# First stage of a hybrid backbone step: load order, filter network kept in one piece, h modulated on ScalarE

## The chip, the cores and the metric

The kernel runs on one core of a Trainium2 chip. The metric is the device time of one execution in microseconds (us); the time before is the median of three runs.

## The reference

One layer of an inference step for 640 tokens of width 1024: 128 context tokens ("prompt", row 0 of `x_tok`) and 512 latent tokens. What the first stage has to produce is the modulated input and the Hyena filters:

```
mod   = silu(cond) @ ada_w + ada_b                  # 6 x 1024: shift1, scale1, gate1, ...
h     = x * (1 + scale1) + shift1
proj  = h @ w_in                                    # q, two gates, v, g, Hyena's three, two mixing gates
hf    = sin(freq0*(z@w1+b1)); hf = sin(freq1*(hf@w2+b2)); hf = sin(freq2*(hf@w3+b3))
filt  = (hf @ w4) * window                          # forward and backward filters, 1024 channels
K     = spectrum(filt)                              # later used as U * K in the long convolution
```

After it come the HGRN2 scan, the short and long convolutions, two projections, the mixing, a layer norm, a SwiGLU network of width 2816 and a second layer norm. All in float32; matmuls are done as three passes over high and low parts (`hi*hi`, `hi*lo`, `lo*hi`).

## The kernel before

The first stage is written out as a list of short tokens, `PLAN`, which `start()` walks through; a scheduler then places the instructions on the five engines, in an order that follows the list where nothing is missing. Each engine runs its own instructions in that fixed order, so one that waits holds up all behind it. All loads stand in SyncE's queue (`SPq`), but for small parameters, which GpSimd issues (token `p`).

The tokens that matter here: `x0` to `x4` load 128 tokens each, `T0` to `T4` transpose them on TensorE and copy the result out of PSUM (`xT`). `mlp` is the filter network (`filter_mlp`): three layers, each a small matmul and then four VectorE steps and a sine on ScalarE (`sin_layer`). `L0` to `L3` load the last filter matrix `w4` and the window for 256 channels (`kern_load`), `A0` to `A3` (`kern_a`) make the filter (matmuls `ks`, product with the window `af`, high and low parts `abh`, `abl`), `B0` to `B3` (`kern_b`) its spectrum by matmuls with the table `kth`, `ktl`, which `k0` to `k2` load and split (`ktab`). `D0` to `D3` load two pieces of 1 MB of `ada_w` for one block of the modulation, `M0` to `M3` multiply and transpose them (`ada_mods`, result `modT`). `h0` to `h7` (`make_h`) modulate 128 rows of x and split them into `hTh` and `hTl`; `HMOD` says which engine modulates (V is VectorE, S is ScalarE), `HSUB` which engine forms the low part (G is GpSimd). `W0` to `W3` store the spectra (`kern_store`, issued from ScalarE's queue). `V0` and `V1` are the first two units of `h @ w_in` (`v_unit`), `m` and the tokens after it the next stage, whose first matmul writes `ma` (line 675).

Buffers tie these together. `xs` has three buffers for five loads, `win` two (the input of the filter network, `zT`, takes one of them first), `araw` three, `raw` three (the `kt` loads use them before the weights do), `af` two. The spectra of blocks 0 and 1 are kept in the buffers that later hold the high (`wh`) and low (`wl`) parts of the weights, three of each, until they have been stored. A PSUM bank of the tag `x` (five) goes from use to use.

Of the kernel before, what the change touches and what calls it, by code (L numbers as in the profile page):

```python
# [12 lines left out]
AF = mybir.ActivationFunctionType  # L13
# [4 lines left out]
P = 128  # L18
# [99 lines left out]

PLAN = """x0 k0 L0 k1 x4 k2 p mlp t L1 T0 x3 T4 A0 x2 D0 T2 A1 x1 L2 B0 M0 T1 D2 A2 M2 T3 h0 L3 B1 D1 A3 h1 B2 M1 D3 h2 h3 M3 h4 W2 W0 h5 h6 h7 W1 q V0 e0 B3 g0 W3 V1 m w0 e2 10 20 g1 50 11 60 g2 70 21 30 40 w1 w2 61 51 52 12 71 Q8 62 22 g3 w3 13 41 g4 53 72 Q9 42 31 63 w4 g5 23 14 w5 73 Z4 Q10 43 32 g6 w6 64 24 15 54 74 Q11 33 65 25 44 16 26 55 75 Q12 Z5 g7 34 w7 66 45 56 17 76 Q13 35 67 46 g8 27 57 w8 18 77 Z6 Q14 g9 g10 36 w9 28 19 68 37 29 58 78 Q15 69 47 59 w10 79 Q16 38 110 210 Z7 g11 610 49 111 510 39 48 w11 211 g12 611 112 w12 212 710 Q17 g13 511 711 Q18 410 113 w13 311 612 Z8 310 411 512 712 Q19 513 213 613 412 713 312 413 313 Z9"""
HMOD = "SVSSVSSS"  # L120
HSUB = "GVVVVGVG"
# [42 lines left out]
def body(tc, I, O):  # L164
# [5 lines left out]
    def act(out, in_, func, bias=0.0, scale=1.0):  # L170
        r = S.activation(out, in_, func, bias=bias, scale=scale)  # L171
        if func in TABLE_FUNCS:
            if last_table[0] is not None:
                tc.add_manual_dep(
                    r.ins, last_table[0].name,
                    mybir.DependencyInfo(mybir.DependencyClass.NoSync, mybir.DependencyReason.DATA),
                    reason="table order")
            last_table[0] = r.ins
        return r

    def tt(out, a, b, op, eng=None):
# [271 lines left out]

    def x_transpose(t, xs):
        for q in range(2):
            ps = sc_bank(f"xT{t}_{q}")
            for k in range(4):
                PE.transpose(ps[:, k * P:k * P + P], xs[:, (4 * q + k) * P:(4 * q + k + 1) * P], ident)
            for i in range(2):
                cpy("x", 2 * t + q, xT.tiles[2 * q + i][:, :, t * P:t * P + P],  # L460
                    ps[:, i * 256:i * 256 + 256].rearrange("p (k t) -> p k t", k=2))
# [14 lines left out]


    def sin_layer(psrc, i, nm):
        a = se.tile([P, HT], F32, tag="af", bufs=2, name=f"sa{nm}")
        V.tensor_scalar(a, psrc, fpar[:, 3 + i:4 + i], fpar[:, 6 + i:7 + i], ALU.add, ALU.mult)  # L480
        k = sp.tile([P, HT], F32, tag="ko", bufs=1, name=f"sk{nm}")
        V.tensor_scalar(k, a, MAGIC, None, ALU.add)
        V.scalar_tensor_tensor(a, k, MAGIC, a, ALU.subtract, ALU.subtract)
        V.tensor_scalar(a, a, HALF, -HALF, ALU.min, ALU.max)
        act(a, a, AF.Sin, scale=-TWO_PI)
        return a
# [243 lines left out]
    def start():  # L730
# [1062 lines left out]
```

## Time and profile before

| what | us |
|---|---|
| median of three runs | 1416.66 (1416.07 to 1417.04) |
| the profiled execution | 1414.7 |
| its span, first to last instruction | 1412.6 |
| TensorE matmuls busy | 1371.9 (97%) |
| VectorE busy | 995.5 (70%) |
| ScalarE busy | 620.8 (44%) |
| GpSimd busy | 63.4 (4%) |

The page divides the span into 40 slices. TensorE is full in nearly all of them but the first two, which are the stage of this change: 5 and 9 tenths, with weight loads at 2 and 6. GpSimd works almost only there (4, 3 and 3 tenths in the first three slices). In the page PE is TensorE, PEld its weight loads, DVE VectorE, ACT ScalarE, POOL GpSimd; a busy PE is not PE at its peak, since matmuls overlap.

### The profile page before, as it was taken

What the parts mean: (1) busy time and instruction counts of PE and PEld (TensorE: products, weight loads), DVE (VectorE), ACT (ScalarE), POOL (GpSimd) and SP (SyncE); (2) the same over time, 40 slices, a digit from 0 to 9 for tenths busy, and PEclk for the clock granted to TensorE, in tenths of its full rate; (3) what the DMA queues carried; (4) which work ended last, traced back from release to release, by engine and by line L of the source; (5) the groups of instructions that cost most, each with busy time, mean ns of one, the idle gap of its engine ahead of it and who ended that gap; (6) DMA issues with size and microseconds to landing.
All of it is one profiled execution on the core that took longest, in us unless ns stands there. A gap on an engine that the chain in (4) does not pass through costs nothing. (4 is left out here: it accounts for less than half of the span.)

```text
span 1412.6 us, 23432 instructions
## 1 busy us (share of the span) xinstructions
PE 1371.9 (97%) x9513; PEld 1291.7 (91%) x9513; DVE 995.5 (70%) x1751; ACT 620.8 (44%) x1011; POOL 63.4 (4%) x56
## 2 busy tenths in 40 slices
PE   5989999999999999999999999998999999999997
PEld 2689889999999999999999999987999999998886
DVE  6886776656889743558887786568987776765426
ACT  3655554432322211546656655327654444542121
POOL 4330000020000000000000000000000000000003
PEclk9999999999999999999999999999999999999999
DMA  7944665675333374433222223552553213267211
GB/s 244 339 139 145 214 212 180 194 245 176 94 86 98 112 231 142 137 94 90 78 87 72 77 60 108 192 172 84 163 149 106 81 58 117 80 210 263 75 60 75
DMA packets 198857, 195.64 MB, mean 138 GB/s; under 512 B 7582, under 2 KB 155774, under 8 KB 197981
## 3 DMA queue, kind: packets, MB, share of 16 engines
q1 hardware_dynamic: 194860, 179.75, 40.6%
q0 software_dynamic: 2160, 9.15, 1.7%
q10 hardware_dynamic: 1728, 5.24, 0.9%
q8 instruction: 74, 1.21, 0.4%
q14 instruction: 35, 0.28, 0.1%
HBM read 162.91 MB, written 31.21 MB: 137 GB/s over the span
## 5 line engine op out<-in xcount | busy, mean ns | idle before, releaser
L182 DVE TENSOR_TENSOR wl<-raw,wh 128x1024 fp32r<-128x1024 f32 x96 | 117.3, 1223 | 133.3 <-ACT wh L358 132.5
L358 ACT CAST wh<-raw 128x1024 fp32r<-128x1024 f32 x90 | 94.1, 1049 | 220.1 <-PE pb L612 41.0
L1431 PE MATMUL fo<-wh,act 128*128 128x512 f32 (+1 forms) x440 | 130.6, 380 | 0.0
L1431 PEld LDWEIGHTS fo<-wh,act 128*128 128x128 f32 x440 | 81.2, 188 | 15.9
L1431 PE MATMUL fo<-wl,act 128*128 128x512 f32 (+1 forms) x220 | 83.4, 379 | 0.0
L612 PE MATMUL hy<-hTh,wh 128*128 128x320 f32 x256 | 79.6, 311 | 0.0
L612 PE MATMUL hy<-hTh,wl 128*128 128x320 f32 x256 | 79.1, 309 | 0.0
L612 PE MATMUL hy<-hTl,wh 128*128 128x320 f32 x256 | 79.1, 309 | 0.0
L612 PE MATMUL f<-hTh,wh 128*128 128x320 f32 x224 | 70.7, 316 | 0.0
L612 PE MATMUL f<-hTl,wh 128*128 128x320 f32 x224 | 69.7, 311 | 0.0
L612 PE MATMUL f<-hTh,wl 128*128 128x320 f32 x224 | 69.2, 309 | 0.0
L182 POOL TENSOR_TENSOR y<-y,gb 128x512 f32<-128x512 f32 x8 | 11.6, 1452 | 891.2 <-ACT y L171 890.9
L1431 PEld LDWEIGHTS fo<-wl,act 128*128 128x128 f32 x220 | 41.3, 188 | 7.9
L612 PEld LDWEIGHTS hy<-hTh,wh 128*128 128x128 f32 x256 | 48.1, 188 | 0.0
L612 PEld LDWEIGHTS hy<-hTl,wh 128*128 128x128 f32 x256 | 48.1, 188 | 0.0
L612 PEld LDWEIGHTS hy<-hTh,wl 128*128 128x128 f32 x256 | 48.1, 188 | 0.0
L171 ACT ACT_TABLE_LOAD x36 | 46.2, 1283 | 1.4 <-PEq L1777 0.7
L715 PE MATMUL v<-wh,hTl 128*128 128x256 f32 x160 | 45.1, 284 | 1.4 <-POOL hTl L182 1.4
L715 PE MATMUL v<-wl,hTh 128*128 128x256 f32 x160 | 44.8, 284 | 1.6 <-DVE wl L182 1.6
L715 PE MATMUL v<-wh,hTh 128*128 128x256 f32 x160 | 44.6, 283 | 0.0
L612 PEld LDWEIGHTS f<-hTl,wh 128*128 128x128 f32 x224 | 42.2, 188 | 0.0
L612 PEld LDWEIGHTS f<-hTh,wh 128*128 128x128 f32 x224 | 42.2, 188 | 0.0
(2292 smaller groups left out, 4699.3 us busy)
## 6 DMA issues: line engine op xcount, KB each, us to landing
raw<-in_w_in SPq DMA_DIRECT2D x52, 512.0 KB, 4.0
araw<-in_ada_w SPq DMA_DIRECT2D x20, 1024.0 KB, 6.2
rm<-in_w_in SPq DMA_DIRECT2D x28, 512.0 KB, 4.6
rp<-in_ffn_w_in SPq DMA_DIRECT2D x24, 512.0 KB, 5.8
raw<-in_ffn_w_out SPq DMA_DIRECT2D x22, 512.0 KB, 4.7
rf<-in_ffn_w_in SPq DMA_DIRECT2D x18, 512.0 KB, 5.0
sd<-my SPq DMA_DIRECT2D x28, 320.0 KB, 2.3
kk<-kd SPq DMA_DIRECT2D x20, 256.0 KB, 2.7
```

The source lines that it names most:

```text
L171: r = S.activation(out, in_, func, bias=bias, scale=scale)
L182: return (eng or V).tensor_tensor(out=out, in0=a, in1=b, op=op)
L358: (V.tensor_copy if HIE[i] == "V" else S.copy)(hi, raw)
L612: r = PE.matmul(ps[:, 0:HT], w[a][:, k, :], x[b][:, k, c0:c0 + HT], start=k == 0 and i == 0, stop=k == kt - 1 and i == 2)
L715: PE.matmul(ps[:, (t - t0) * 256:(t - t0) * 256 + 256], hT[b][:, k, t * P:t * P + P], w[a][:, k % 4, :], start=k == 0 and i == 0, stop=k = ...
L1431: PE.matmul(ps, x(t, b, k0 + kk), w[a][:, kk, :], start=first and kk == 0 and i == 0, stop=last and kk == nk - 1 and i == 2)
```

## The change

`PLAN` is rewritten from its start to `B3`; from `g0` on it is the same. `x4` is loaded second and the filter network comes before the tables `k0` to `k2`, which follow the first pair of `ada_w` loads. The blocks of the modulation are loaded and multiplied in the order 0, 2, 1, 3 as before, but block 2 comes ahead of the second filter block's spectrum, and h0 to h3 ahead of block 1. `HMOD` names ScalarE for all eight blocks of h. The casts of the table all go to ScalarE. Four instructions get an explicit place on their engine: x0's first transpose after the second layer's matmul `f2`, the casts of the table after the third layer's first sine, and the first block's sums `wsd` after the second layer's last VectorE step. `filter_mlp` therefore does the transposes of x0 itself.

```diff
--- before.py
+++ after.py
@@ -116,8 +116,8 @@
     return {k: np.ascontiguousarray(v) for k, v in c.items()}
 
 
-PLAN = """x0 k0 L0 k1 x4 k2 p mlp t L1 T0 x3 T4 A0 x2 D0 T2 A1 x1 L2 B0 M0 T1 D2 A2 M2 T3 h0 L3 B1 D1 A3 h1 B2 M1 D3 h2 h3 M3
...
-HMOD = "SVSSVSSS"
+PLAN = """x0 x4 L0 p mlp L1 x3 T4 t D0 A0 k0 k1 k2 T3 x2 x1 T2 A1 M0 D2 T1 B0 L2 M2 D1 h0 h1 h2 h3 A2 B1 L3 D3 M1 M3 B2 A3
...
+HMOD = "SSSSSSSS"
 HSUB = "GVVVVGVG"
 WSUB = "VGGVVGGG"
 TAILPOS = 1
@@ -139,7 +139,7 @@
 PHB = 2
 GB = 3
 PSA2 = dict(mm=("mm", 4), sc=("x", 4), o=("x", 4), tr=("x", 4))
-COPIES = {'x': 'SSVSSSSSSS', 'h': 'SSSSSSSV', 'm': 'SV', 'k': 'VSS', 'w': 'SVVS', 'v': 'VSSS', 'a': 'SSSSSSSSSVVSSSSSSSSS', 'o': 'SSSSSSSSVSSS'}
+COPIES = {'x': 'SSVSSSSSSS', 'h': 'SSSSSSSV', 'm': 'SV', 'w': 'SVVS', 'v': 'VSSS', 'a': 'SSSSSSSSSVVSSSSSSSSS', 'o': 'SSSSSSSSVSSS'}
 ASUB = "GVVVGVGVGGGGVGVGVVVG"
 KSUB = "GGG"
 HP = False
@@ -177,6 +177,13 @@
                     reason="table order")
             last_table[0] = r.ins
         return r
+
+    def order_after(ins, prev):
+        if prev is not None:
+            tc.add_manual_dep(
+                ins.ins, prev.ins.name,
+                mybir.DependencyInfo(mybir.DependencyClass.NoSync, mybir.DependencyReason.DATA),
+                reason="issue order")
 
     def tt(out, a, b, op, eng=None):
         return (eng or V).tensor_tensor(out=out, in0=a, in1=b, op=op)
@@ -451,11 +458,13 @@
         SY.dma_start(xs, x_tok[t])
         return xs
 
-    def x_transpose(t, xs):
+    def x_transpose(t, xs, after=None):
         for q in range(2):
             ps = sc_bank(f"xT{t}_{q}")
             for k in range(4):
-                PE.transpose(ps[:, k * P:k * P + P], xs[:, (4 * q + k) * P:(4 * q + k + 1) * P], ident)
+                x = PE.transpose(ps[:, k * P:k * P + P], xs[:, (4 * q + k) * P:(4 * q + k + 1) * P], ident)
+                if q == 0 and k == 0:
+                    order_after(x, after)
             for i in range(2):
                 cpy("x", 2 * t + q, xT.tiles[2 * q + i][:, :, t * P:t * P + P],
                     ps[:, i * 256:i * 256 + 256].rearrange("p (k t) -> p k t", k=2))
@@ -475,14 +484,16 @@
         tt(hTl[:, k, :], xT[:, k, :], f32(hTh[:, k, :]), ALU.subtract, G if HSUB[k] == "G" else V)
 
 
+    net = {}
+
     def sin_layer(psrc, i, nm):
         a = se.tile([P, HT], F32, tag="af", bufs=2, name=f"sa{nm}")
         V.tensor_scalar(a, psrc, fpar[:, 3 + i:4 + i], fpar[:, 6 + i:7 + i], ALU.add, ALU.mult)
         k = sp.tile([P, HT], F32, tag="ko", bufs=1, name=f"sk{nm}")
         V.tensor_scalar(k, a, MAGIC, None, ALU.add)
         V.scalar_tensor_tensor(a, k, MAGIC, a, ALU.subtract, ALU.subtract)
-        V.tensor_scalar(a, a, HALF, -HALF, ALU.min, ALU.max)
-        act(a, a, AF.Sin, scale=-TWO_PI)
+        net["clamp", nm] = V.tensor_scalar(a, a, HALF, -HALF, ALU.min, ALU.max)
+        net["sin", nm] = act(a, a, AF.Sin, scale=-TWO_PI)
         return a
 
     hf_hi = sp.tile([P, T], F32R, name="hf_hi")
@@ -490,7 +501,7 @@
     kth = sp.tile([P, 2304], F32R, name="kth")
     ktl = sp.tile([P, 2304], F32R, name="ktl")
 
-    def filter_mlp():
+    def filter_mlp(xs0):
         ps = sc_bank("f1")
         for hf in range(2):
             PE.matmul(ps[hf * ORD:hf * ORD + ORD, 0:HT], w1, zT[:, hf * HT:hf * HT + HT], start=True, stop=True)
@@ -498,8 +509,9 @@
         ps = sc_bank("f2")
         for hf in range(2):
             cs = slice(hf * ORD, hf * ORD + ORD)
-            PE.matmul(ps[cs, 0:HT], w2[cs], h1[cs], start=True, stop=True)
+            net["f2"] = PE.matmul(ps[cs, 0:HT], w2[cs], h1[cs], start=True, stop=True)
         h2 = sin_layer(ps[:, 0:HT], 1, "2")
+        x_transpose(0, xs0, net["f2"])
         V.memset(hf_lo[ORD:P, :].bitcast(F32), 0.0)
         for hf in range(2):
             ps = sc_bank(f"f3_{hf}")
@@ -514,7 +526,7 @@
         cs = slice(i * 768, i * 768 + 768)
         raw = wp.tile([P, 768], F32, tag="raw", bufs=RAW_BUFS, name=f"kt{i}")
         SY.dma_start(raw, I["kt"][:, cs])
-        cpy("k", i, kth[:, cs], raw)
+        order_after(S.copy(kth[:, cs], raw), net["sin", "31"])
         tt(ktl[:, cs], raw, f32(kth[:, cs]), ALU.subtract, G if KSUB[i] == "G" else V)
 
     def kern_load(cc):
@@ -531,8 +543,10 @@
         c0 = cc * 256
         w4, win, skp = loaded
         wsd = se.tile([P, 2, 256], F32, tag="wsd", name=f"wsd{cc}")
-        tt(wsd[:, 0], w4[:, 0], w4[:, 1], ALU.add)
-        tt(wsd[:, 1], w4[:, 0], w4[:, 1], ALU.subtract)
+        for i, op in enumerate((ALU.add, ALU.subtract)):
+            x = tt(wsd[:, i], w4[:, 0], w4[:, 1], op)
+            if cc == 0:
+                order_after(x, net["clamp", "2"])
         whi = se.tile([P, 2, 256], F32R, tag="whi", name=f"whi{cc}")
         cpy("w", cc, whi, wsd)
         whl = se.tile([P, 2, 256], F32R, tag="whl", bufs=1, name=f"whl{cc}")
@@ -597,13 +611,6 @@
     def kern_store(cc, out):
         for t, f, n in out:
             KQ.dma_start(kd[cc, :, f:f + n], t)
-
-    def order_after(ins, prev):
-        if prev is not None:
-            tc.add_manual_dep(
-                ins.ins, prev.ins.name,
-                mybir.DependencyInfo(mybir.DependencyClass.NoSync, mybir.DependencyReason.DATA),
-                reason="issue order")
 
     def dense_fm(w, x, half, ps, kt=KT, after=None):
         c0 = half * HT
@@ -773,11 +780,7 @@
 
         for tok in PLAN.split():
             if tok == "mlp":
-                if HP:
-                    with tc.high_priority():
-                        filter_mlp()
-                else:
-                    filter_mlp()
+                filter_mlp(xs[0])
                 continue
             step(tok[0], int(tok[1:] or 0))
 
```

Lines of `PLAN` are cut at `h4`; the rest of each is the same.

The order of instructions on an engine, as the scheduler set it, differs at these places. First SyncE's queue of loads at the start; `xs` are pieces of x, `kt` of the table, `w4` and `win` a filter block's matrix and window, `araw` pieces of `ada_w`. Before:

```order
L516 DMA kt0_141<-in_kt 128x768
L524 DMA w4_0_145<-in_filt_w4 64x2x256 x2
L527 DMA win0_148<-in_win 128x5x256
L516 DMA kt1_150<-in_kt 128x768
L451 DMA xs4_154<-in_x_sample 128x1024
L516 DMA kt2_156<-in_kt 128x768
L524 DMA w4_1_224<-in_filt_w4 64x2x256 x2
L527 DMA win1_227<-in_win 128x5x256
L451 DMA xs3_243<-in_x_sample 128x1024
L451 DMA xs2_316<-in_x_sample 128x1024
```

Now:

```order
L458 DMA xs4_141<-in_x_sample 128x1024
L536 DMA w4_0_143<-in_filt_w4 64x2x256 x2
L539 DMA win0_146<-in_win 128x5x256
L536 DMA w4_1_217<-in_filt_w4 64x2x256 x2
L539 DMA win1_220<-in_win 128x5x256
L458 DMA xs3_222<-in_x_sample 128x1024
L405 DMA araw0_0_247<-in_ada_w 128x4x512
L405 DMA araw0_1_249<-in_ada_w 128x4x512
L528 DMA kt0_308<-in_kt 128x768
L528 DMA kt1_312<-in_kt 128x768
L528 DMA kt2_316<-in_kt 128x768
L458 DMA xs2_334<-in_x_sample 128x1024
```

The three `kt` moved behind the first two `araw`, x4 and the second filter block's loads moved ahead, and x2, the last of the first piece, now follows the `kt`.

GpSimd at the end of the stage; `wl1` and `wl2` are low parts of weights for the v units, `hTl3` the low part of the last pair of h's blocks, `abl3` the low parts of the last filter block. Before:

```order
L182 TENSOR_TENSOR abl2_3_554<-af2_3_551,abh2_3_553 128x512
L182 TENSOR_TENSOR wl1_926<-raw1_923,wh1_925 128x1024
L182 TENSOR_TENSOR wl2_932<-raw2_929,wh2_931 128x1024
L182 TENSOR_TENSOR abl3_0_702<-af3_0_697,abh3_0_701 128x512
L182 TENSOR_TENSOR hTl2_873<-xT2_131,hTh2_872 128x640
L182 TENSOR_TENSOR abl3_4_740<-af3_4_737,abh3_4_739 128x512
L182 TENSOR_TENSOR hTl3_889<-xT3_132,hTh3_888 128x640
```

Now:

```order
L189 TENSOR_TENSOR abl2_3_612<-af2_3_609,abh2_3_611 128x512
L189 TENSOR_TENSOR abl3_0_831<-af3_0_826,abh3_0_830 128x512
L189 TENSOR_TENSOR hTl2_873<-xT2_131,hTh2_872 128x640
L189 TENSOR_TENSOR hTl3_889<-xT3_132,hTh3_888 128x640
L189 TENSOR_TENSOR abl3_4_869<-af3_4_866,abh3_4_868 128x512
L189 TENSOR_TENSOR wl1_926<-raw1_923,wh1_925 128x1024
L189 TENSOR_TENSOR wl2_932<-raw2_929,wh2_931 128x1024
```

The two `wl` moved behind `hTl3` and the last `abl3`.

ScalarE's queue in the same part; `kd` are the stores of the spectra, `ko1` those of block 1, `wh0` to `wh2` high parts of weights, `hTh` high parts of h. Before:

```order
L185 CAST hTh1_842<-xT1_130 128x640
L185 CAST abh2_4_562<-af2_4_560 128x512
L599 DMA kd_66<-ko1_p_618 128x512
L599 DMA kd_66<-ko1_0_648 128x1024
L418 COPY md3_861<-ada3_852 128x512
L599 DMA kd_66<-ko1_1_679 128x1024
L358 CAST wh0_919<-raw0_917 128x1024
L358 CAST wh1_925<-raw1_923 128x1024
L358 CAST wh2_931<-raw2_929 128x1024
```

Now:

```order
L192 CAST abh3_1_841<-af3_1_837 128x512
L613 DMA kd_66<-ko2_0_781 128x1024
L192 CAST abh3_2_850<-af3_2_848 128x512
L192 CAST hTh3_888<-xT3_132 128x640
L192 CAST abh3_3_859<-af3_3_857 128x512
L171 ACTIVATE xT3_132<-xT3_132,modT_119 128x128
L171 ACTIVATE xT3_132<-xT3_132,modT_119 128x512
L613 DMA kd_66<-ko1_p_631 128x512
L613 DMA kd_66<-ko1_0_661 128x1024
L192 CAST abh3_4_868<-af3_4_866 128x512
L613 DMA kd_66<-ko2_1_812 128x1024
L613 DMA kd_66<-ko1_1_692 128x1024
```

The stores of `ko1` stood ahead of the first `wh`, and now stand behind the last modulation of h (`xT3`), mixed with those of block 2.

## Rows read from the trace of the kernel before

**Rows 1.** Windows: stretch, us, busy of PE, PEld, DVE, ACT, POOL (instructions); clock, DMA share, GB/s

```profile
20.00:66.00 46.00, 41.48 (x260) 28.42 (x258) 41.89 (x90) 28.07 (x60) 14.92 (x10) 0.96 0.94 326
66.00:88.00 22.00, 17.56 (x140) 16.40 (x137) 18.16 (x32) 13.94 (x22) 12.40 (x6) 1.00 0.51 172
88.00:114.00 26.00, 26.00 (x220) 26.00 (x219) 24.26 (x39) 13.52 (x22) 0.00 (x0) 1.00 0.32 118
114.00:200.00 86.00, 84.72 (x561) 76.58 (x560) 65.97 (x98) 48.19 (x82) 0.00 (x0) 1.00 0.63 199
```

**Rows 2.** Timeline, PE: start us, length us, engine, line, operation [idle before <- what ended it]

```profile
8.73 1.33 PE L501 MATMUL f<-sa,w 64*64 64x320 f32 x4 [2.49 <-ACT sa L171]
17.34 1.44 PE L507 MATMUL f<-sa,w 64*128 64x320 f32 x4 [7.28 <-ACT sa L171]
...
18.87 3.44 PE L458 MATMUL xT<-cst,xs 128*128 128x128 f32 x16
...
87.16 0.39 PE L715 MATMUL v<-wh,hTl 128*128 128x256 f32 x1 [0.66 <-POOL hTl L182]
...
114.09 0.31 PE L675 MATMUL ma<-hTh,wmg0h 128*128 128x320 f32 x1
```

**Rows 3.** Timeline, DVE, the filter network

```profile
6.29 0.61 DVE L480 TENSOR_SCALAR sa<-f,fpar 128x320 f32<-128x320 f32 x1 [0.91 <-PE f L496]
...
7.85 0.33 DVE L484 TENSOR_SCALAR sa<-sa 128x320 f32<-128x320 f32 x1
...
13.08 0.76 DVE L182 TENSOR_TENSOR wsd<-w 128x256 f32<-128x256 f32 x2 [2.38 <-DMA w<-in_filt_w]
...
18.81 0.61 DVE L480 TENSOR_SCALAR sa<-f,fpar 128x320 f32<-128x320 f32 x1 [2.28 <-PE f L507]
...
20.75 1.45 DVE L484 TENSOR_SCALAR sa<-sa 128x320 f32<-128x320 f32 x1
...
24.49 0.69 DVE L182 TENSOR_TENSOR af<-ks,win 128x512 f32<-128x512 f32 x1
```

**Rows 4.** Timeline, ACT, a sine and a copy of x

```profile
16.82 0.46 ACT L171 ACTIVATE sa<-sa 128x320 f32<-128x320 f32 x1
...
22.67 0.35 ACT L185 COPY xT<-xT 128x256 f32<-128x256 f32 x1
```

**Rows 5.** Lines, DVE, 0 to 120 us: group, count, busy us, mean ns, idle before

```profile
L469 DVE TENSOR_SCALAR xT<-xT,modT 128x128 f32<-128x128 f32 (+1 forms) x4 | 4.7, 1187 | 0.1
```

**Rows 6.** Timeline, DVE, around the end of the stage

```profile
69.59 1.22 DVE L182 TENSOR_TENSOR wl<-raw,wh 128x1024 fp32r<-128x1024 f32 x1
...
76.89 0.69 DVE L182 TENSOR_TENSOR af<-ks,win 128x512 f32<-128x512 f32 x1 [3.53 <-POOL abl L182]
...
84.28 0.48 DVE L185 CAST hTh<-xT 128x640 fp32r<-128x640 f32 x1
...
85.61 1.52 DVE L182 TENSOR_TENSOR lbm<-prT 128x16 f32<-128x16 f32 x1
...
98.63 1.22 DVE L182 TENSOR_TENSOR wl<-raw,wh 128x1024 fp32r<-128x1024 f32 x1
```

**Rows 7.** Timeline, POOL

```profile
20.18 1.83 POOL L182 TENSOR_TENSOR ktl<-kt,kth 128x768 fp32r<-128x768 f32 x1 [1.37 <-ACT kth L185]
...
70.11 5.50 POOL L182 TENSOR_TENSOR wl<-raw,wh 128x1024 fp32r<-128x1024 f32 x2 [6.32 <-DMA kd<-ko]
...
81.50 1.58 POOL L182 TENSOR_TENSOR abl<-af,abh 128x512 fp32r<-128x512 f32 x1 [0.56 <-ACT abh L185]
84.90 2.20 POOL L182 TENSOR_TENSOR hTl<-xT,hTh 128x640 fp32r<-128x640 f32 x1 [1.83 <-DVE hTh L185]
```

**Rows 8.** Windows, the first 29 us, columns as in rows 1

```profile
0.00:29.00 29.00, 13.21 (x48) 8.42 (x48) 17.28 (x47) 10.19 (x22) 14.88 (x23) 0.94 0.84 263
```

**Rows 9.** Timeline, SyncE's queue, the fourth window's load

```profile
45.29 0.55 SPq L527 DMA_DIRECT2D win<-in_win  x1
```

**Rows 10.** DMA issues of 0 to 130 us: what, count, size, median us to landing

```profile
kd<-ko ACTq DMA_DIRECT2D x8, 512.0 KB, 4.5
```

More of the change, by code (lines that the diff above doesn't have):

```diff
@@ L116, in _constants @@
     return {k: np.ascontiguousarray(v) for k, v in c.items()}
-PLAN = """x0 k0 L0 k1 x4 k2 p mlp t L1 T0 x3 T4 A0 x2 D0 T2 A1 x1 L2 B0 M0 T1 D2 A2 M2 T3 h0 L3 B1 D1 A3 h1 B2 M1 D3 h2 h3 M3 h4 W2 W0 h5 h6 h7 W1 q V0 e0 B3 g0 W3 V1 m w0 e2 10 20 g1 50 11 60 g2 70 21 30 40 w1 w2 61 51 52 12 71 Q8 62 22 g3 w3 13 41 g4 53 72 Q9 42 31 63 w4 g5 23 14 w5 73 Z4 Q10 43 32 g6 w6 64 24 15 54 74 Q11 33 65 25 44 16 26 55 75 Q12 Z5 g7 34 w7 66 45 56 17 76 Q13 35 67 46 g8 27 57 w8 18 77 Z6 Q14 g9 g10 36 w9 28 19 68 37 29 58 78 Q15 69 47 59 w10 79 Q16 38 110 210 Z7 g11 610 49 111 510 39 48 w11 211 g12 611 112 w12 212 710 Q17 g13 511 711 Q18 410 113 w13 311 612 Z8 310 411 512 712 Q19 513 213 613 412 713 312 413 313 Z9"""
-HMOD = "SVSSVSSS"
+PLAN = """x0 x4 L0 p mlp L1 x3 T4 t D0 A0 k0 k1 k2 T3 x2 x1 T2 A1 M0 D2 T1 B0 L2 M2 D1 h0 h1 h2 h3 A2 B1 L3 D3 M1 M3 B2 A3 h4 W2 W0 h5 h6 h7 W1 q V0 e0 B3 g0 W3 V1 m w0 e2 10 20 g1 50 11 60 g2 70 21 30 40 w1 w2 61 51 52 12 71 Q8 62 22 g3 w3 13 41 g4 53 72 Q9 42 31 63 w4 g5 23 14 w5 73 Z4 Q10 43 32 g6 w6 64 24 15 54 74 Q11 33 65 25 44 16 26 55 75 Q12 Z5 g7 34 w7 66 45 56 17 76 Q13 35 67 46 g8 27 57 w8 18 77 Z6 Q14 g9 g10 36 w9 28 19 68 37 29 58 78 Q15 69 47 59 w10 79 Q16 38 110 210 Z7 g11 610 49 111 510 39 48 w11 211 g12 611 112 w12 212 710 Q17 g13 511 711 Q18 410 113 w13 311 612 Z8 310 411 512 712 Q19 513 213 613 412 713 312 413 313 Z9"""
+HMOD = "SSSSSSSS"
 HSUB = "GVVVVGVG"
```

## Prediction

> **What bounds the kernel now.** I read the busy times by stretch first [rows 1]. From 88 to 114 us TensorE works through all 26 us; from 66 to 88 it has 17.6 of 22, from 20 to 66 only 41.5 of 46, much of it stretched (its weight loads fill just 28.4). TensorE's own rows [rows 2] then give the instant that matters: the next stage opens at 114.09 with the first matmul of `ma`. From there the change leaves TensorE's order as good as alone, and TensorE is busy 84.7 of the next 86 us [rows 1]. So the change is worth what it moves 114.09.
>
> What holds 114.09 is read backwards from it. At 87.16 TensorE waits for GpSimd's last `hTl`, and from there 224 matmuls by the order run without a gap: 26.93 / 224 = 0.12 each. That `hTl` (84.90, 2.20 long [rows 7]) follows VectorE's cast of `hTh`, block 7, at 84.28, which ends at 84.76 [rows 6]. I call the end of this cast the hinge. VectorE gets to the hinge late for four reasons, all in its rows: the filter network's chain is cut by casts and weight sums that wait for loads [rows 3]; four modulations of h run on it [rows 5]; it waits 3.53 for GpSimd at 76.89, whose two `wl` had just held it for 5.50 [rows 6, 7]; and between 20 and 66 it is simply full, 41.9 of 46 [rows 1].
>
> **What the change takes away, counted to the hinge.**
>
> Filter chain. Before, the second sine starts from the matmul `f2` at 8.73 (1.33 long, ends 10.06), but VectorE stands behind a cast of `kth` and the sums `wsd`, which wait 2.38 for their load; the third layer's first VectorE step comes at 18.81 [rows 2, 3]. Now nothing stands there. The four VectorE steps of a layer take 6.29 to 8.18 = 1.89, so they end at 11.95. Eight transposes of x0 now sit on TensorE between `f2` and `f3`: half of 3.44 = 1.72, to 11.8; three copies of theirs stand ahead of the sine on ScalarE, the last of 0.35 to 12.2; the sine 0.46 to 12.6 [rows 4]; `f3` 1.44 to 14.0. `wsd` (0.76) now comes just ahead of the third layer and costs about 0.2. So the third layer starts 4.6 earlier. I carry 4.3 to the first `af` (24.49 before), since `whl`'s two steps now queue inside this layer; the ones that go are as long. Gain 4.3; between 3 and 5.
>
> Modulations. Four VectorE instructions go, 4.7 in all [rows 5]; two of them were stretched by GpSimd. ScalarE gets four more. It has 28.1 of 46 busy from 20 to 66 and 13.9 of 22 after [rows 1], so that is covered, except where it stands in h's own chain (below). Gain 4.7.
>
> GpSimd's two `wl` now come after the hinge, so the wait of 3.53 goes; VectorE's own `wl` (1.2, at 69.59) moves behind the hinge too. Gain 4.7 together.
>
> Sum of gains: 4.3 + 4.7 + 4.7 = 13.7; the hinge would come at 71.1.
>
> **What it adds before the hinge.**
>
> The three `kt` loads move behind the first ada_w pair, so GpSimd's `ktl` (1.8 each, [rows 7]) fall at about 29 to 36, where VectorE is full. What one costs VectorE is seen at 20.75: a step of 0.33 took 1.45 beside a `ktl`, so 1.1 [rows 3, 7]. Zero of three to all three in full length: 0 to 5.4, of which 1.1 was paid before. I take two at 1.1, less that one: +1.1.
>
> x2 is loaded behind `kt`, and the second filter block (`ks1`) now stands behind x2's transposes on TensorE. The loads up to x2 are by their shapes 7.56 MB, the same set that came with the first ada_w pair before; 29 us at 263 GB/s are 7.6 MB [rows 8]. So x2 is there at 29 to 31, its transposes and the first `ks1` at 32, while VectorE is free at 30.4. I take +1.5, between 0 and 3.
>
> Block 2's last `abh` stands on ScalarE behind the cast of the first `raw`, which lands after all of ada_w, and the last filter block (`ks3`) now stands on TensorE behind all of block 2's kernel matmuls. VectorE has nothing else ahead of `ks3`. I take +2.4, between 0 and 4.
>
> The queue of loads: SyncE still holds the load of `win3` until VectorE has read `win1`, 45.29 before [rows 9]. By the steps above that is again near 45. But only two ada_w loads stand behind it now and four did before. The last ada_w pair should land some 5 us sooner; that is what lets the other gains through, and nothing to add.
>
> Sum: 71.1 + 1.1 + 1.5 + 2.4 = 76.1 for the hinge; before 84.76.
>
> **From the hinge to `ma`.** Here it gives most back. Before it took 114.09 - 84.76 = 29.3. Now GpSimd has to do after the hinge, in this order, `hTl` of block 7, the last `abl`, and both `wl`. TensorE is by then only at the last kernel block; its 13th matmul of the v stage wants the first of those `wl`, and 240 matmuls (28.8 us) are left at it. GpSimd: 2.20 for `hTl` (its wait for one VectorE step included), 1.58 for `abl`, 5.50 / 2 = 2.75 for `wl` [rows 7], and about 0.5 more since VectorE's `wl` of 1.2 starts first: 7.0. TensorE's route is so 7.0 + 28.8 = 35.8.
> VectorE's route: the third v load's low part (`wl`, at 98.63, ends 99.85) came 15.1 after the hinge. Now six steps of about 0.75 and a `wl` of 1.2 come ahead of it that had been done or came later, two of about 0.65 and the 1.4 lost at 85.61 go: 15.1 + 5.7 - 2.7 = 18.1. Behind it 106 matmuls, 12.7. That is 30.8 if GpSimd never holds VectorE up, and 37.8 if all its 7.0 us do. I take 36.8 for both routes together, nearer the upper end because of the row at 85.61: 0.1 us of work took 1.52.
> `ma` then opens at 76.1 + 36.8 = 112.9, 1.2 sooner. The profiled execution took 1414.7 (span 1412.6 and 2.1 around it), 2.0 below the median of the runs, 1416.66. So 1413.5 against the profile, and 1415.5 for the median.
>
> **Rivals.**
>
> A, faster. None of the three additions shows, the hinge comes at 71 to 74, and `ma` at 108 to 111: gain 3 to 6, 1411 to 1413.5. For it: VectorE's waits before the hinge were all of the kind that the change removes. Against: it needs GpSimd's seven microseconds after the hinge to be short as well.
>
> B, slower, by GpSimd and VectorE keeping each other out. Two rows look like it: 1.45 for a step of 0.33 beside a `ktl`, and 1.52 for 128x16 elements beside the last `hTl` [rows 3, 6, 7]. If every `ktl` costs VectorE its full 1.8, the hinge moves by 5.4 - 2.2 = 3.2 to 79.3, and the tail is 37.8: `ma` at 117.1, 3.0 later, 1419.7. It decides from a hinge at about 76.3 on (114.1 - 37.8).
> The Trainium skill's page "SBUF — State Buffer" (section "SBUF: two separate sides") states this as a rule: VectorE instructions with two SBUF inputs and GpSimd's hold the shared port in turn, each for its whole length, and the other waits. Rows at 85.61 and 20.75 agree; by the rule the time would be this rival's.
>
> C, slower or even, by the stores. The first two blocks' outputs lie in the buffers of `wh` and `wl`, so every `wl` needs a store to land; GpSimd's idle 6.3 before 70.11 is that wait [rows 7]. On ScalarE's queue block 1's stores now stand behind all of h, at about 74 and not at 64. With the 4.5 us that such stores take to land [rows 10], the first is there at 78.5; VectorE wants its `wl` at 76.3. That stops VectorE for 2 (4 if the queue is full), its route decides, and `ma` comes at 76.1 + 37.8 + 2 to 4 = 115.9 to 117.9: 1418.5 to 1420.5.
>
> D, the change doesn't do what it says: `win3` still waits for its buffer with loads behind it, the last ada_w pair comes at 64 again, and ScalarE, TensorE and VectorE wait for it as before: 1416.5.
>
> **How the numbers follow.** My forecast, 1415.5 and within 0.2% (2.8 us, what a measurement here can tell from no change): chance 0.34, own range 1413.9 to 1418. D 0.08, also no change. A 0.32. B 0.14, nearly all of it beyond 0.2%; C 0.12, a little over half beyond. So faster 0.32, same 0.48, slower 0.20. The range is 1410.8 to 1420.0: at the lower end the hinge at 71 and the tail as taken, at the upper B and most of C.
>
> **What would show it.** In the new profile: the third layer's first step near 14 and the first `af` near 20; no modulation on VectorE; the cast of block 7 near 76; GpSimd's two `wl` after it, to 83 or 86; TensorE idle for a microsecond early in the v stage and again at its second half; `ma` near 113. A hinge above 79, or a `wl` of VectorE's that waits for a DMA, proves me wrong towards slower; a hinge below 74 and a tail under 36 towards faster. Were `ma` sooner and the time not, something after this stage would have given it back, and my reading of the next stage as full would be the error.

## The result, and the profile after

| | us (median of 4 runs) | profiled span | first `ma` | span behind it |
|---|---|---|---|---|
| before | 1416.41 (1416.07 to 1417.04) | 1412.6 | 114.09 | 1298.5 |
| after | 1425.29 (1424.58 to 1427.37) | 1423.2 | 122.84 | 1300.4 |

The ratio is 1.0063, 95% interval 1.0051 to 1.0076: slower by 8.9 us, outside the range that I gave. Of the 10.6 us between the two profiled spans 8.75 lie ahead of the first matmul of `ma`. The profiled execution of the kernel before was one of its quick ones (1414.7, 1.7 below its median), so 10.6 is some 2 us too large as the price of the change.

By stretch, in the profile after (columns as in [rows 1]):

```profile
20.00:66.00 46.00, 39.53 (x263) 27.96 (x262) 38.41 (x74) 28.37 (x54) 18.82 (x12) 0.94 0.93 326
66.00:88.00 22.00, 15.88 (x87) 13.65 (x86) 18.55 (x32) 14.12 (x24) 8.34 (x5) 0.82 0.40 144
88.00:114.00 26.00, 24.00 (x180) 23.79 (x179) 24.18 (x32) 10.17 (x16) 7.38 (x2) 0.89 0.36 117
```

Against [rows 1] TensorE has 87 matmuls from 66 to 88 where it had 140, and its granted clock is 0.82 and 0.89 where it was 1.00. The timelines of the four engines there; first TensorE:

```profile
87.23 0.58 PE L600 MATMUL k<-abl,kth 128*128 128x256 f32 x1 [2.71 <-POOL abl L189]
...
92.50 0.39 PE L722 MATMUL v<-wl,hTh 128*128 128x256 f32 x1 [2.00 <-POOL wl L189]
...
122.84 0.31 PE L682 MATMUL ma<-hTh,wmg0h 128*128 128x320 f32 x1
```

VectorE, the filter network, then the end of the stage:

```profile
13.46 1.13 DVE L491 TENSOR_SCALAR sa<-f,fpar 128x320 f32<-128x320 f32 x2
...
19.35 0.69 DVE L189 TENSOR_TENSOR af<-ks,win 128x512 f32<-128x512 f32 x1
...
33.58 2.40 DVE L189 TENSOR_TENSOR af<-af 1x256 f32<-1x256 f32 x2
...
70.43 1.29 DVE L189 TENSOR_TENSOR af<-ks,win 128x512 f32<-128x512 f32 x2 [3.41 <-issue]
...
82.01 0.48 DVE L192 CAST hTh<-xT 128x640 fp32r<-128x640 f32 x1
...
82.61 1.21 DVE L189 TENSOR_TENSOR wl<-raw,wh 128x1024 fp32r<-128x1024 f32 x1
...
93.05 2.35 DVE L189 TENSOR_TENSOR lbe<-lbe,lbe 128x16 f32<-128x16 f32 x1
```

GpSimd:

```profile
82.63 2.64 POOL L189 TENSOR_TENSOR hTl<-xT,hTh 128x640 fp32r<-128x640 f32 x1 [6.16 <-DVE hTh L192]
85.23 1.95 POOL L189 TENSOR_TENSOR abl<-af,abh 128x512 fp32r<-128x512 f32 x1
87.14 8.23 POOL L189 TENSOR_TENSOR wl<-raw,wh 128x1024 fp32r<-128x1024 f32 x2
```

ScalarE's queue of stores:

```profile
78.52 0.33 ACTq L613 DMA_DIRECT2D kd<-ko_p  x1
78.89 0.45 ACTq L613 DMA_DIRECT2D kd<-ko  x1
82.13 0.81 ACTq L613 DMA_DIRECT2D kd<-ko  x2
```

By the order in the section on the change, the first two of these stores and the last one are block 1's. They came at 63.4 to 66.6 before:

```profile
63.38 0.33 ACTq L599 DMA_DIRECT2D kd<-ko_p  x1
63.74 0.44 ACTq L599 DMA_DIRECT2D kd<-ko  x1
66.55 0.33 ACTq L599 DMA_DIRECT2D kd<-ko  x1
```

Their buffers become the three `wl`, so VectorE's `wl0` is made at 82.61 (69.59 before) and GpSimd's two at 87.14 to 95.37 (70.11 to 75.61 before, [rows 6, 7]). Before the last `hTl` came TensorE had done 66 of v's 240 matmuls (174 of the 224 behind 87.16 are v's); now it has done 6 of them when it gets there, and waits instead. No `wl` of the changed kernel waits for a store in the trace: the stores landed 2.0 to 2.6 us after their issue, VectorE's `wl` follows its last copy at once, and GpSimd's follow its `abl`. The late stores act through the order that the scheduler made of them, in which all three `wl` stand behind the hinge.

How 122.84 comes about: the cast of block 7 ends at 82.49; GpSimd's route to the matmul that wants its first `wl` takes 10.0, to 92.50; the 240 matmuls that I had counted from there need 28.8; and 1.5 are lost because the stretch after the wait ran slow. Sum 122.8.

### The profile page after: what moved, and what is told of

Read it like the earlier page. It is cut to its first block, busy times and chain, and to the rows that moved or that the text cites. A ratio compares the mean times of both kernels' runs of the same rounds, so it can differ in the third digit from the quotient of the medians.

```text
span 1423.2 us, 23434 instructions
## 1 busy us (share of the span) xinstructions
PE 1377.6 (97%) x9513; PEld 1297.4 (91%) x9513; DVE 999.3 (70%) x1746; ACT 624.2 (44%) x1016; POOL 67.0 (5%) x56
```

## The experiments

Theory A, formed from these rows: the order of the list puts block 1's stores behind block 2's and behind h's modulations on ScalarE; they hold the buffers of all `wl`; so v's matmuls cannot fill TensorE's waits and come in one piece behind the hinge (the end of VectorE's cast of block 7, as in the prediction). Rivals: B, GpSimd and VectorE keeping each other out; C, `ks3` behind kernel block 2; D, the modulations on ScalarE themselves; E, TensorE's half clock; F, the stores themselves.

One ledger for all runs, from windows that end at the first `ma`. "Idle" is TensorE's idle time ahead of it (length less busy time). "Clock" is a rough measure: the length of each of three stretches (0 to 20, 20 to 66, 66 to the first `ma`) times (1 - granted clock). The first `ma` is the sum of the two and 86 to 92 us in every kernel (97 in e6, which has 9 us of added matmuls). The ledger says where the time stands, not what put it there.

Each ratio is to executions of the kernel before that were taken with the run, whose medians lie between 1416.3 and 1417.7; so ratios are compared, and not the us of two rows. The last four columns come from one execution each, and executions of one kernel differ by a few us (spans of 1412.5 to 1418.2 in 26 of the kernel before), so 1 to 3 us in them say nothing alone. In e3, e9 and e13 "clock" is some 2 us too low (see the last section).

| run | us | ratio to before, interval | first `ma` | idle | clock | behind `ma` |
|---|---|---|---|---|---|---|
| before | 1416.41 | | 114.09 | 23.5 | 1.8 | 1298.5 |
| after | 1425.29 | 1.0063 (1.0051 to 1.0076) | 122.84 | 26.2 | 10.4 | 1300.4 |
| e1 | 1412.54 | 0.9957 (0.9942 to 0.9972) | 110.84 | 18.4 | 3.2 | 1298.4 |
| e2 | 1423.46 | 1.0040 (1.0026 to 1.0055) | 121.47 | 25.4 | 9.8 | 1299.2 |
| e3 | 1412.69 | 0.9960 (0.9946 to 0.9975) | 112.18 | 21.1 | 0.0 | 1298.3 |
| e4 | 1416.59 | 0.9993 (0.9983 to 1.0003) | 114.34 | 20.5 | 5.4 | 1299.4 |
| e5 | 1431.14 | 1.0092 (1.0077 to 1.0107) | 128.19 | 33.4 | 8.7 | 1301.6 |
| e6 | 1430.55 | 1.0093 (1.0076 to 1.0110) | 125.28 | 23.3 | 5.1 | 1303.4 |
| e7 | 1416.40 | 0.9991 (0.9982 to 1.0001) | 117.11 | 24.4 | 5.1 | 1298.1 |
| e8 | 1419.70 | 1.0015 (1.0006 to 1.0025) | 116.54 | 21.1 | 7.0 | 1303.3 |
| e9 | 1418.66 | 1.0017 (1.0007 to 1.0028) | 117.65 | 24.2 | 1.6 | 1299.1 |
| e10 | 1420.54 | 1.0026 (1.0015 to 1.0037) | 118.26 | 24.9 | 7.0 | 1300.0 |
| e11 | 1422.35 | 1.0036 (1.0021 to 1.0051) | 123.67 | 26.3 | 10.4 | 1298.0 |
| e12 | 1420.56 | 1.0022 (1.0012 to 1.0032) | 119.61 | 27.7 | 3.5 | 1298.2 |
| e13 | 1426.90 | 1.0067 (1.0050 to 1.0084) | 121.66 | 26.1 | 3.3 | 1303.2 |

**e1, stores early.** After, with one token moved:

```diff
-... B2 A3 h4 W2 W0 h5 h6 h7 W1 q V0 ...
+... B2 A3 W1 h4 W2 W0 h5 h6 h7 q V0 ...
```

> Block 1's three stores to kd are placed ahead of blocks 2's and 0's in the table, nothing else is edited; the scheduler then puts them 30 rows earlier on ScalarE's queue and GpSimd's two wl ahead of the last two halves of h. Theory A (the stores came at 78.52 to 82.13 us, held the buffers of wl1 and wl2, GpSimd made both after the hinge at 82.49, and v's matmuls could neither fill TensorE's idle stretches nor start before 92.50): wl1 is made before 78 us, v fills the stretches before the hinge, the first ma matmul opens at hinge + 29 to 31, 112 to 114, and the run ends at 1413 to 1417 us. Rival B (what costs is GpSimd and VectorE keeping each other out, wherever the two wl lie): the 4 us move ahead of the hinge, 1420 to 1423. Rival C (ks3 behind kernel block 2) and rival D (all modulations on ScalarE) see no change: 1424 to 1426.

As A said, or a little better, and 0.43% faster than before; only the way from the hinge was shorter than A had it (23.7, not 29 to 31). `ks3` still stands behind kernel block 2 here, and all modulations are on ScalarE, so C and D, which saw no change, fall as the cause by themselves. By stretch:

```profile
66.00:88.00 22.00, 20.38 (x155) 19.02 (x153) 17.83 (x33) 14.28 (x24) 10.50 (x6) 1.00 0.50 180
```

GpSimd's timeline:

```profile
67.53 2.55 POOL L189 TENSOR_TENSOR wl<-raw,wh 128x1024 fp32r<-128x1024 f32 x1 [3.00 <-ACT wh L365]
...
76.88 2.42 POOL L189 TENSOR_TENSOR wl<-raw,wh 128x1024 fp32r<-128x1024 f32 x1 [1.61 <-ACT wh L365]
```

VectorE's:

```profile
66.58 1.22 DVE L189 TENSOR_TENSOR wl<-raw,wh 128x1024 fp32r<-128x1024 f32 x1
...
86.70 0.49 DVE L192 CAST hTh<-xT 128x640 fp32r<-128x640 f32 x1
```

The hinge is at 87.19, 4.7 later than in the changed kernel, and `ma` 12.0 earlier: TensorE had done 57 of v's matmuls by 88.46 and stood still for 1.6 us between 66 and 88, not 6.1. The edit also moved other steps of VectorE; e9 and e13 separate them.

**e2, both `wl` on VectorE.**

```diff
-WSUB = "VGGVVGGG"
+WSUB = "VVVVVGGG"
```

> The two low halves wl1 and wl2 move from GpSimd to VectorE, stores left where they are. Rival B: VectorE makes each in 1.2 us and its steps after the hinge lose their stretch (mb x2 3.71 and lbe 2.35 where 1.6 and 0.2 stand in the kernel before), so nearly all of the loss after the hinge goes: 1418 to 1421 us. Theory A: wl1 still waits for the store issued at 78.89 and landed some 4 us later, v still starts only then, at 87 to 90 instead of 92.50: 1420 to 1423. C and D: 1424 to 1426.

Just above A's range: 0.23% come back by the ratios, whose intervals overlap, and 2.5 us by the spans (1420.7). As far as these two `wl` go, B is no more than that. v's matmuls start at 88.95, behind an `abl` that took GpSimd 3.08 beside VectorE's `wl`.

**e3, ks3 first.**

```diff
-... B2 A3 h4 W2 W0 ...
+... A3 B2 h4 W2 W0 ...
```

> A3 stands ahead of B2 in the table, so that TensorE makes ks3 before kernel block 2, as in the kernel before. The scheduler then puts two of block 1's stores earlier and wl1 ahead of h's last low halves on GpSimd, and leaves the third store and wl2 late. Rival C: VectorE's 3.4 us wait at 67 us and TensorE's idle stretches from 72 to 76 go, hinge near 79, all of the loss but the late wl2 goes: 1415 to 1419 us. Theory A: wl1 early lets v's first half start, wl2 late holds its second unit only, so about half to two thirds of the loss goes too: 1416 to 1421; what separates them is where TensorE's idle time before the hinge goes. B: 1423 to 1425. D: 1425.

As good as e1, below both ranges. It doesn't tell A from C, since it also moved `wl0` to 66.55 and GpSimd's first `wl` to 71.97. e1 is the run against C; e8 was to add the two edits, and missed both expectations.

**e4, modulation undone.**

```diff
-HMOD = "SSSSSSSS"
+HMOD = "SVSSVSSS"
```

> Only the modulation string goes back to the one of the kernel before, so that blocks 1 and 4 of h are modulated by VectorE. Rival D (ScalarE carries too much): 1416 to 1420 us. Theory A: it only matters through the order that comes out, in which wl1 is ahead of the last low halves on GpSimd and wl2 behind: 1417 to 1422, with the first wl made before the hinge and v's matmuls filling the stretch before it. C: ks3 still stands behind kernel block 2: 1424 to 1426. B: 1423 to 1426.

In D's range, just below A's, and no different from before. With VectorE's modulations back, ScalarE issues most of block 1's stores earlier, `wl0` is made at 65.38 and GpSimd's first `wl` at 67.41; its second comes at 87.61.

**e5, late stores in the kernel before.**

```diff
...
-            KQ.dma_start(kd[cc, :, f:f + n], t)
+            st[cc] = KQ.dma_start(kd[cc, :, f:f + n], t)
+            if cc == 1:
+                order_after(st[cc], st[2])
```

> The kernel before, with one constraint: block 1's stores to kd are issued behind block 2's last. Nothing of the change is in it. The scheduler then puts GpSimd's two wl behind the last low half of h, as in the changed kernel. Theory A (late stores are enough by themselves to bring the loss): both wl only after the hinge, TensorE idle and then at half its clock between 70 and 95 us, first ma matmul at 121 to 125 where it stands at 114.09, 1422 to 1428 us. Rival D (the loss comes from ScalarE's longer row of modulations or from another part of the change): no more than 2 us, 1416 to 1419.

More than A expected: 13.8 us, with nothing of the change in the kernel. Late stores are enough to bring such a loss. Its size is not that of the change, since the three stores come later here (86.5 to 88.5). GpSimd's timeline, where a `wl` does wait for a store:

```profile
90.94 5.34 POOL L182 TENSOR_TENSOR wl<-raw,wh 128x1024 fp32r<-128x1024 f32 x2 [2.17 <-DMA kd<-ko]
```

TensorE's:

```profile
97.42 0.58 PE L719 MATMUL v<-wl,hTh 128*128 128x256 f32 x1 [8.28 <-DVE wl L182]
```

**e6, TensorE's waits filled.** After, with 75 repeats of a v matmul into unread columns (17 beside `ks3`, 24 behind the last `hTh`, 34 ahead of the first use of `wl1`):

```diff
...
+            f = PE.matmul(net["spare"], hTh[:, k, 0:P], net["wh0"], start=True, stop=True)
+            order_after(f, prev)
...
```

> The changed kernel with 75 more matmuls of 256 columns, into columns of a bank that nobody reads, placed where TensorE waits between 72 and 92 us, so that it has no long idle stretch there; the stores stay late. In the changed kernel the stretches 76 to 84, 86 to 92 and 94 to 98 ran at a granted clock of 0.50 to 0.73. Rival E (the half clock is the loss: 12 us from the first experiment's ma to this one's, of which 5.5 are busy time of the same matmuls): the granted clock is 1.00 from 66 to 114 and the run ends at 1418 to 1421. Theory A (wl1, not to be had before 91 to 92.5, sets when the bulk of v starts; most of the slow matmuls lie ahead of that and are covered by it): the clock rises as well, but only the 1.4 to 1.7 us that v lost after 94 come back, 1422.5 to 1425.

Neither. The clock rose, the time did not fall. By stretch:

```profile
66.00:88.00 22.00, 18.90 (x135) 16.70 (x134) 18.55 (x33) 14.27 (x24) 8.26 (x4) 1.00 0.41 144
88.00:114.00 26.00, 24.01 (x189) 23.80 (x187) 24.72 (x30) 10.02 (x15) 8.31 (x3) 0.93 0.27 83
```

TensorE's timeline:

```profile
93.36 0.39 PE L739 MATMUL v<-wl,hTh 128*128 128x256 f32 x1 [1.99 <-POOL wl L190]
```

From 66 to 88 there is no slow stretch left, and v still has to wait for GpSimd's `wl`, until 93.36 now (GpSimd's last `hTl` and `abl` took 3.46 and 4.27 ahead of it, 2.64 and 1.95 in the changed kernel; why, no run tests). So E falls as the main cause: the half clock before 88 lay under waits. What the slow stretch behind 92.50 cost, 1.5 us, is not tested here, since e6 has one too. The span is even 5.5 longer: 2.4 at `ma`, since the low half came 0.9 later and part of kernel block 3 behind v, and 3.0 in the next stage, for reasons that I did not test.

**e7, modulation alone**, on the kernel before:

```diff
-HMOD = "SVSSVSSS"
+HMOD = "SSSSSSSS"
```

> The kernel before with h's modulation all by ScalarE and nothing else. The scheduler leaves two of block 1's stores where they were, puts the third behind block 2's second, and wl2 behind the last low half of h on GpSimd; wl1 stays early. Theory A: as in the experiment with the modulation undone, where wl1 was early and wl2 late, most of v can fill TensorE; 0 to 3 us slower than before, 1416 to 1419. Rival D (the modulations themselves make the loss): 1421 to 1425. My prediction's own step (4.7 us off VectorE comes through to the end): 1412 to 1414.

At A's lower end: no different from before. D falls as a cause by itself: the same edit costs 0.7% on top of the rest of the change (e4 to after) and nothing alone.

**e8, both orders.**

```diff
-... B2 A3 h4 W2 W0 h5 h6 h7 W1 q V0 ...
+... W1 A3 B2 h4 W2 W0 h5 h6 h7 q V0 ...
```

> The changed kernel with block 1's stores ahead in the table and A3 ahead of B2, the two edits that gained 12 us each by themselves. Theory A: both removed the same thing, TensorE's idle time and half clock between 70 and 95 us, and of it 1.6 and 1.5 us of idle time are left between 66 and 88 us; so no more than 1.5 us on top: 1411 to 1413. Rival C (ks3's place is a cause of its own): the two gains add up at least in part, 1406 to 1410.

A miss for both: 0.6% (some 8 us) slower than either edit alone, and A as it stood does not cover it. All `wl` are early, but v's first matmuls now stand ahead of `ks3`. VectorE's timeline:

```profile
67.30 2.54 DVE L189 TENSOR_TENSOR whl<-wsd,whi 64x512 fp32r<-64x512 f32 x1 [0.24 <-ACT whi L192]
```

TensorE's:

```profile
69.99 0.76 PE L558 MATMUL ks<-whl,hf_hi 128*128 128x512 f32 x1 [0.46 <-DVE whl L189]
```

That `whl` ran beside GpSimd's `wl` (66.82, 2.47 long) and took 2.54. The ten matmuls of `ks3` took 4.4 us, at a granted clock of 0.50 (70 to 74) behind several short waits; in e1 they took 6.3 with 31 of v's among them. Another slow stretch after `ma`, at 132 to 138 (0.51), is part of the 4.9 us that it loses there against e1; its profiled execution was its slowest, 2.2 above its median.

**e9, wl1 and wl2 held.** e1, with the two behind h's last low half on GpSimd:

```diff
...
+            if i in (1, 2):
+                order_after(x, net["low"])
...
```

> The first experiment's kernel (stores early) with one more constraint: GpSimd makes wl1 and wl2 only behind the last low half of h, though their buffers are free long before. Theory A (late wl is the direct agent, the stores act only through it): v has its first 36 to 40 matmuls early, the rest after the hinge and both wl, with VectorE's strided sums beside them; 1419 to 1426 us, at least 7 above the first experiment. Rival F (late stores act by themselves, through ScalarE's queue or the DMA traffic to kd, and wl's place is harmless): 1412 to 1415.

Just below A's range, and far from F's. 0.60% (8.5 us) of the 1.06% between e1 and after come back with two low halves alone, block 1's stores left early. F falls for that part. The first v matmul that wants `wl1`:

```profile
91.74 0.39 PE L724 MATMUL v<-wl,hTh 128*128 128x256 f32 x1 [4.65 <-POOL wl L189]
```

**e10, ks3 first and all stores early.**

```diff
-... B2 A3 h4 W2 W0 h5 h6 h7 W1 q V0 ...
+... A3 B2 h4 W1 W2 W0 h5 h6 h7 q V0 ...
```

> A3 ahead of B2 and all three of block 1's stores ahead of block 2's and 0's, but behind h4 in the table, so that v does not stand ahead of ks3 on TensorE as in the combination before, where ks3 waited 0.5 us for whl at 70 and ran at half the clock. Theory A: what the first and the third experiment removed is the same, so 1411 to 1414 us. If early wl's on GpSimd cost as much beside VectorE as they give (rival B): 1416 to 1420.

Missed by A as well, and just above B's range. Here v's first half stands ahead of kernel block 3, and TensorE waits for the low parts of h; the wait before 91.12 ended with GpSimd's last one, and 90 to 98 ran at 0.56 to 0.58:

```profile
84.25 0.39 PE L722 MATMUL v<-wh,hTl 128*128 128x256 f32 x1 [1.61 <-POOL hTl L189]
...
91.12 0.58 PE L722 MATMUL v<-wh,hTl 128*128 128x256 f32 x1 [1.89 <-POOL hTl L189]
```

So early low halves are needed for the gain, and are not enough for it: TensorE must also have other work while h's last block is made. That second condition is read from e8 and e10 afterwards; no run tests it.

**e11, the filter chain alone**, on the kernel before (`filter_mlp`, `x_transpose` and `wsd` as in the change, table and modulations as before).

> The kernel before with the filter network's chain kept together (x0's transposes behind the second layer, block 0's sums behind the second clamp) and nothing else: its table of loads and its modulations stay. My prediction's step: 4.3 us earlier on VectorE, all through to the end: 1412 to 1413.5. Theory A: TensorE's first stretch opens earlier, but what follows waits for loads and for GpSimd's wl, wl2 moves behind h's last low half; 1414 to 1419.

Slower than even A allowed. TensorE waits 10.4 us for `whl` of blocks 0 to 2, and the loads come later; SyncE's queue, the last two `ada_w` pairs:

```profile
49.41 13.57 SPq L405 DMA_DIRECT2D araw<-in_ada_w  x4
```

Issued until 62.98, 56.5 before. The loss shows in these waits and in the slow matmuls behind them (granted clock 0.85 from 20 to 66, 0.84 from 66 to 88); why the loads moved I did not test. Nor does this run price the filter chain as it is in the change: the first `af`, 19.35 there and 24.49 before, stands here at

```profile
25.17 0.69 DVE L189 TENSOR_TENSOR af<-ks,win 128x512 f32<-128x512 f32 x1 [0.31 <-PE ks L559]
```

**e12, the loads alone**, on the kernel before: the new `PLAN`, with `T0` put back ahead of `t`.

> The kernel before with the new table of loads and nothing else. My prediction's step (wl waits and the last ada_w pair, some 5 us): 1411 to 1414. Theory A: its order stands close to that of the experiment with the modulation undone (1416.6 there), with the filter network slower; wl1 early, wl2 late: 1416 to 1420.

Just above A's range, far from mine. Alone, the three parts give +0.36%, +0.22% and nothing; the chain and the loads together (e4) nothing; all three +0.63%. A fourth part, the table's casts on ScalarE, is in e4 but in neither e11 nor e12.

**e13, all three low halves held.** e9, with `wl0` also behind VectorE's cast of h's last block:

```diff
...
-            if i in (1, 2):
-                order_after(x, net["low"])
+            if i < 3:
+                order_after(x, net["low" if i else "high"])
...
```

> As the run that held wl1 and wl2, and wl0 as well, behind VectorE's cast of h's last block; stores early as in the first experiment. TensorE's order comes out as in the changed kernel, v's bulk behind kernel block 3. Theory A in its full form (block 1's three late stores hold the buffers of all three wl: wl0, made by VectorE at 67 us in the first experiment and at 82.61 in the changed kernel, carries the half of the loss that holding wl1 and wl2 alone did not bring back): 1423 to 1427 us, first ma matmul at 121 to 124. Rival F (the other half comes from the stores themselves or from another part of the change): 1418 to 1420, as with two held.

In A's range, and the changed kernel's ratio again. VectorE's and GpSimd's rows:

```profile
86.92 1.21 DVE L189 TENSOR_TENSOR wl<-raw,wh 128x1024 fp32r<-128x1024 f32 x1
...
89.52 5.91 POOL L189 TENSOR_TENSOR wl<-raw,wh 128x1024 fp32r<-128x1024 f32 x2
```

e1 and e13 have the same list and block 1's stores within about 1 us of the same places; holding three low halves is worth 1.10% (15.6 us), 0.50% of it by `wl0`. F falls: the stores act through these buffers. That the ratio is the same is in part luck: 10.8 us of the loss against e1 lie ahead of `ma` (12.0 in the changed kernel), the rest behind it.

**All runs together.** I counted in TensorE's rows how many of v's matmuls it had done by the hinge: 6 in after, e2, e5 and e13, and 42 to 63 in all others (e6 aside, where added matmuls look like v's). With 6 done, the first `ma` comes 34.7 to 41.7 us after the hinge; with 42 or more, 23.7 to 31.0. The hinge itself still counts: in e11 it comes at 94.96, and `ma` at 123.67 with 63 done.

## Why the prediction was wrong

The first `ma` came at 122.84 and not at 112.9. Of these 9.9 us 6.4 came with the hinge and 3.5 behind it.

- **Filter chain.** Right: the third layer at 13.46, the first `af` at 19.35 (I said 14 and 20). It did not reach the end: from the first `af` to the hinge VectorE now takes 63.1 us, 60.3 before.
- **Modulations.** None is left on VectorE, and its `wl` stands behind the hinge, 6.0 us less work. Yet it is busy for 52.1 us between the first `af` and the hinge, 52.3 before. Most of it went to the same steps, in the same number, taking longer: ten `abl` 9.6 instead of 7.7, five `wsd` 3.0 instead of 2.0, three `whl` 3.0 instead of 2.1, sixteen steps on the one-row `af` 8.7 instead of 7.3. The long ones ran beside a GpSimd instruction; the `wsd` at 55.31 took 1.43 while GpSimd's `abl` ran from 55.05 to 56.47. Two of the modulations that went had been stretched like this (2.63 at 70.73, 1.43 at 53.89), and other steps took their place. That is a reading of the rows; no run isolates it. In e7, where I counted on 4.7 us, the ratio gained 0.09%, with an interval that reaches zero.
- **The hinge.** 82.49, not 76.1. VectorE's busy time from 20 to 66 fell from 41.9 to 38.4, and the difference turned into waiting: I had taken a full engine for the bound of the stretch. Of my additions, `ks3` cost 3.41 where I took 2.4, x2 1.19 where I took 1.5, and two steps beside GpSimd's `ktl` were stretched by some 2.7, 1.6 net of the 1.1 paid before, where I took 1.1 (33.58: two of 0.41 took 2.40; an `abl` at 28.95 took 1.77 instead of 0.69). The last ada_w pair was issued 7.6 sooner (48.9, 56.5 before), but its block left TensorE only 2.3 sooner, not 5, as ScalarE's copies of it show, before and now:

```profile
66.49 0.59 ACT L418 COPY md<-ada 128x512 f32<-128x512 f32 x1 [2.52 <-PE ada L407]
```

```profile
64.17 0.59 ACT L425 COPY md<-ada 128x512 f32<-128x512 f32 x1
```

- **From the hinge to `ma`.** 40.35, not 36.8. The 240 matmuls were right. GpSimd's route took 10.0 where I had 7.0, and the slow stretch behind its wait 1.5, which no step of mine had; 1.0 of it I had allowed above TensorE's route.
- **The step that failed.** By size, it is the sum up to the hinge, where 8.7 us of gain were to come and 2.3 came, and then the tail. By mechanism, it is the backward reading under both: the end of the cast plus a tail that I had priced apart. e1's hinge is later than the changed kernel's and its `ma` 12 us earlier. The hinge alone does not set `ma`; how much of v TensorE has done while it would otherwise wait counts for more. I had the facts: the tail counts 240 matmuls left, and rival C names the late stores and that every `wl` needs one. I priced C as a stop of VectorE by 2 to 4 us, with the stores at 74; they came at 78.5 to 82.1, no `wl` waited for one, and what stopped was TensorE's filler.
- **Rival B** was in the rows, stronger than I drew it: two `wl` took 8.23 on GpSimd, 5.50 before, and VectorE's 128x16 sum 2.35, 0.16 before:

```profile
89.90 0.16 DVE L182 TENSOR_TENSOR lbe<-lbe,lbe 128x16 f32<-128x16 f32 x1
```

The Trainium skill's page "SBUF — State Buffer" (section "SBUF: two separate sides") says that a VectorE instruction with two SBUF inputs and a GpSimd one that reads SBUF hold their shared port in turn, each for its whole length. These rows agree: the sum ended at 95.40, GpSimd's second `wl` at 95.37. The row at 20.75 that the prediction gives for this rule is a step with one input, so it is no case of the rule as worded there. The price of the two `wl` by e2 is 0.23%, some 3 us; what the sharing costs ahead of the hinge no run prices.
- **Behind `ma`.** 1298.5 became 1300.4; I had taken it as unchanged, and 2 us of a single execution are within its spread. In e6, e8 and e13 it lost 5 us; whether a late or waiting first stage does that was not tested.
- **The range.** A hinge at 71 with the tail as taken gives 1410.4, not the 1410.8 of its lower end; nothing hangs on it.

## What to carry to other kernels

When a bound engine has work that fills its waits, ask of every reordering what that filler needs (here the low halves of weights, and the stores that free their buffers) and where each of these now stands in its queue. Count the bound engine's idle time and filler up to the point that matters, not only the distance from one late instruction. Where a scheduler follows a list, test the parts together: two parts that cost alone cost nothing together, and one that cost nothing alone cost 0.7% with them. Early low halves are no rule by themselves either: e8 and e10 have them, and are 0.15% and 0.26% slower than before. The version to keep is e1: one token moved, 0.43% (0.28 to 0.58) faster than the kernel before.

## What the runs showed of the hardware

TensorE's granted clock fell to 0.50, the 1.2 GHz level, behind waits of 0.76 to 2.71 us, and matmuls of the same shape then came 0.21 us apart instead of 0.12: in the changed kernel the stretches below follow waits of 1.36, 1.02 and 0.76 us in close order, one of 2.71, and one of 2.00.

```profile
80.00:82.00 2.00, 2.00 (x10) 1.78 (x9) 2.00 (x4) 0.16 (x1) 0.00 (x0) 0.50 0.67 272
88.00:90.00 2.00, 2.00 (x12) 2.00 (x11) 2.00 (x4) 0.05 (x1) 2.00 (x1) 0.50 0.00 0
94.00:96.00 2.00, 2.00 (x11) 2.00 (x10) 2.00 (x2) 0.00 (x0) 1.38 (x1) 0.50 0.70 236
```

The rows count ten to twelve matmuls in 2 us, and 19 from 100 to 102, where the clock is 1.00. TensorE is busy for all 2 us in either case, so a slow stretch looks full.

By the matmuls' own durations the record of the granted clock is not complete. In e8 the window from 70 to 74 has 0.50, and a matmul of `ks` takes 0.63:

```profile
70.00:74.00 4.00, 4.00 (x10) 3.13 (x11) 2.62 (x6) 0.04 (x1) 0.00 (x0) 0.50 0.79 269
```

```profile
70.97 0.63 PE L558 MATMUL ks<-whl,hf_hi 128*128 128x512 f32 x1
```

In e9 the first filter block's matmuls of that shape take 0.63 as well, and the window has 1.00:

```profile
20.00:24.00 4.00, 4.00 (x13) 2.46 (x15) 3.44 (x10) 0.62 (x1) 0.97 (x1) 1.00 1.04 387
```

```profile
20.80 0.63 PE L560 MATMUL ks<-whl,hf_hi 128*128 128x512 f32 x1
```

e3 and e13 have the same from 19.1 to 23.7, while e1, whose rows there also show 0.63, is recorded at 0.68. At 1.00 such a matmul takes 0.40 (e1, 70.02). So the duration of a known matmul is the check on the clock row, and these three kernels' "clock" in the ledger is low by some 2 us, an estimate: half of the 4.6 us.
